# Binary cross-entropy on one core: other widths for the first and the last chunk, and another order of VectorE's work at the end

## The chip, the cores and the metric

The kernel runs on one core of one Trainium2 chip. The metric is the device time of one execution in microseconds. Its engines that matter here are VectorE (DVE), ScalarE (ACT), GpSimd (POOL) and SyncE (SP); TensorE has no work. Each engine takes its instructions in program order and waits where an operand isn't ready. Transfers between HBM (the large memory) and SBUF (the memory on the core: 128 partitions) are carried by 16 DMA engines; an engine's instruction issues a transfer, and here POOL issues nearly all of them.

## The reference

```python
def reference(pred, target):          # both 8192 x 8192, float32; target is 0 or 1
    eps = 1e-7
    pred = np.clip(pred, eps, 1 - eps)
    return -(target * np.log(pred) + (1 - target) * np.log(1 - pred))
```

268 MB are read for each of the two inputs, and 268 MB are written. As the target is 0 or 1, the result is -log(p) where it is 1 and -log(1 - p) where it is 0, that is -log(|p + t - 1|).

## The kernel before

The 8192 x 8192 elements are seen as one flat row, cut into 35 chunks. A chunk of width w takes 128 x w elements in a row: each of the 128 partitions holds w neighbouring ones. Chunks 1 to 33 have w = 15360 columns (`WIDE`), chunks 0 and 34 have 8704 (`SIDE`); per partition that makes 524288 columns.

Two buffers stand in SBUF. `ring_p` has three slots of 15360 float32 columns; chunk k lives in slot k mod 3, is loaded there, changed in place and stored from there. `ring_t` has one slot of 15360 columns of 8-bit integers for the target: the DMA reads float32 from HBM and writes 8-bit values, so a target load reads as many bytes as a pred load and writes a quarter.

Each chunk goes through these steps, in two halves (`PARTS`) of its columns:

- `load_p` (line 63) and `load_t` (line 67): loads of pred and target; all on POOL's queue but pred of chunk 0, which is on ACT's.
- `clip` (line 85): VectorE, a two-operation tensor_scalar, in place.
- `merge` (lines 89 to 95): VectorE computes (t - 1) + p (line 91); ScalarE takes the absolute value (line 94) and the logarithm (line 95), all in place.
- `negate` (line 99): VectorE multiplies by -1.
- `store` (line 70), and for the last chunk `store_last` (lines 72 to 81): all columns but the last 1024 in one transfer on POOL (line 74), the last 1024 in three transfers on SP, of 108, 12 and 8 rows (line 77).

The order is written out by hand (lines 101 to 128); a framework only adds the waits that the data needs, by the columns that two instructions share. For chunk k the program takes: merge of both halves; the target load of chunk k + 1, which waits until both merges have read `ring_t`; negate of both halves; clip of both halves of chunk k + 1; the store of chunk k; the pred load of chunk k + 2, which waits until the store of chunk k - 1 has emptied the slot. So POOL's queue is, from the start: t(0), p(1), t(1), store(0), p(2), t(2), store(1), p(3), and so on; an issue that waits holds up all that follow it. The DMA engines take POOL's transfers in the order of their issue.

At the end this changes. The store of chunk 32 isn't issued in its turn, but between the two halves of the target load of chunk 34 (lines 114 to 117): after t(33) and p(34), POOL has t(34, half 0), store(32), t(34, half 1), store(33), and the last store. VectorE takes for the last two chunks: merge(33) in both halves, negate(33) in both halves, clip(34), merge(34), negate(34).

Below p(k), t(k), store(k) are the transfers of chunk k, and merge(k, i), clip(k, i), negate(k, i) VectorE's work on half i.

Of the kernel before, what the change touches and what calls it, by code (L numbers as in the profile page):

```python
# [1 line left out]

# [4 lines left out]

EPS = 1e-7

WIDE = 15360  # L10
SIDE = 8704
SLOTS = 3
PARTS = 2
REST = 1024
ROWS = (108, 12, 8)


@with_exitstack
def kernel(
    ctx: ExitStack,  # L20
    tc: tile.TileContext,
    pred: bass.AP,
    target: bass.AP,
    out: bass.AP,
):
    nc = tc.nc
    fp32 = mybir.dt.float32
    uint8 = mybir.dt.uint8
    Alu = mybir.AluOpType
    Act = mybir.ActivationFunctionType  # L30
    P = nc.NUM_PARTITIONS

    R, C = pred.shape
    total = R * C // P
    n = (total - 2 * SIDE) // WIDE + 2
    widths = [SIDE] + [WIDE] * (n - 2) + [SIDE]
    assert sum(widths) == total
    last = n - 1

    pool = ctx.enter_context(tc.tile_pool(name="rings", bufs=1))  # L40
    ring_p = pool.tile([P, SLOTS * WIDE], fp32, name="ring_p", tag="ring_p")
    ring_t = pool.tile([P, WIDE], uint8, name="ring_t", tag="ring_t")
    warm = pool.tile([1, 8], fp32, name="warm", tag="warm")

    def chunk(ap, k):
        flat = ap.rearrange("r c -> (r c)")
        start = sum(widths[:k]) * P
        return flat[start : start + widths[k] * P].rearrange("(p w) -> p w", p=P)

    def p_of(k, a=0, b=None):  # L50
        c = k % SLOTS * WIDE
        return ring_p[:, c + a : c + (widths[k] if b is None else b)]

    def t_of(k, a=0, b=None):
        return ring_t[:, a : widths[k] if b is None else b]

    def part(k, i):
        w = widths[k]
        return i * w // PARTS, (i + 1) * w // PARTS

    def load_p(k):
        queue = nc.scalar if k == 0 else nc.gpsimd
        queue.dma_start(out=p_of(k), in_=chunk(pred, k))  # L63

    def load_t(k, *cols):
        cols = cols or (0, widths[k])
        nc.gpsimd.dma_start(out=t_of(k, *cols), in_=chunk(target, k)[:, cols[0] : cols[1]])  # L67

    def store(k):
        nc.gpsimd.dma_start(out=chunk(out, k), in_=p_of(k))  # L70

    def store_last():
        w = SIDE - REST
        nc.gpsimd.dma_start(out=chunk(out, last)[:, :w], in_=p_of(last, 0, w))  # L74
        r = 0
        for rows in ROWS:
            nc.sync.dma_start(
                out=chunk(out, last)[r : r + rows, w:], in_=p_of(last, w)[r : r + rows, :]
            )
            r += rows  # L80
        assert r == P

    def clip(k, i):
        p = p_of(k, *part(k, i))
        nc.vector.tensor_scalar(  # L85
            out=p, in0=p, scalar1=EPS, scalar2=1 - EPS, op0=Alu.max, op1=Alu.min
        )

    def merge(k, i):
        p, t = p_of(k, *part(k, i)), t_of(k, *part(k, i))  # L90
        nc.vector.scalar_tensor_tensor(  # L91
            out=p, in0=t, scalar=1.0, in1=p, op0=Alu.subtract, op1=Alu.add
        )
        nc.scalar.activation(out=p, in_=p, func=Act.Abs)  # L94
        nc.scalar.activation(out=p, in_=p, func=Act.Ln)  # L95

    def negate(k, i):
        p = p_of(k, *part(k, i))
        nc.vector.tensor_scalar(out=p, in0=p, scalar1=-1.0, scalar2=None, op0=Alu.mult)  # L99

    with tc.manual_schedule():
        load_p(0)
        load_t(0)
        load_p(1)
        nc.vector.memset(warm, 1.0)  # L105
        nc.scalar.activation(out=warm, in_=warm, func=Act.Ln)  # L106
        for i in range(PARTS):
            clip(0, i)
        for k in range(n):
            for i in range(PARTS):  # L110
                merge(k, i)
            if k < last - 1:
                load_t(k + 1)
            elif k == last - 1:
                load_t(last, 0, SIDE // PARTS)
                store(last - 2)
                load_t(last, SIDE // PARTS, SIDE)
            for i in range(PARTS):
                negate(k, i)
            if k < last:  # L120
                for i in range(PARTS):
                    clip(k + 1, i)
            if k < last - 2:
                store(k)
            if k < last - 1:
                load_p(k + 2)
        store(last - 1)
        store_last()


# [1 line left out]
_INS = ['pred', 'target']  # L132
_OUTS = [((8192, 8192), 'float32')]


# [23 lines left out]
```

## Time and profile before

| | us |
|---|---|
| median of 3 runs (1881.55 to 1883.01) | 1881.91 |
| the profiled execution, its own time | 1882.49 |
| its span, first to last instruction | 1880.5 |
| clip, L85, 7680 columns / 4352 columns, each | 4.16 / 2.42 |
| merge on VectorE, L91, 7680 / 4352, each | 8.15 / 4.68 |
| Abs, L94, and Ln, L95, 7680 / 4352, each | 6.60 / 3.82 |
| negation, L99, 7680 / 4352, each | 4.16 / 2.43 |
| POOL's issue of a target load, L67, mean of 36 | 0.53 |
| POOL's issue of a pred load, L63, mean of 34 | 3.88 |
| POOL's issue of a store, L70, mean of 34 | 3.74 |

The profile lists for each engine when it was busy, what ended its waits, and how busy the DMA engines were. A line of the timeline gives the start, the length, the engine, the line of the code, the operation, output and input by their names in the program, how many alike follow each other, and in brackets the idle time before it with what ended it. A line of the windows gives a stretch of time, its length, the busy time of VectorE, ScalarE and POOL in it (with the number of instructions), the clock, the mean busy share of the 16 DMA engines, and what they wrote in GB/s; a target load shows there with a quarter of the bytes that it reads.

### The profile page before, as it was taken

To read this page: it belongs to the slowest core of one execution; us is meant where nothing else is said; L and a number is where in the kernel's file an instruction comes from. 1 tells how busy PE (TensorE), PEld (TensorE's weight loads), DVE (VectorE), ACT (ScalarE), POOL (GpSimd) and SP (SyncE) were. 2 spreads that over 40 slices of the span, in tenths; PEclk is the share of its full clock that TensorE was granted. 3 is DMA by queue.
4 is the path that set the end of the run, shared out by engine and by line. 5 is a ranking of instruction groups with operands and counts; after the bars stand their busy time and mean duration, and the time that the engine had idled before them with its cause. 6 is when DMAs were issued, how large, how long until landed. Compare 5 with 4: busy or idle time off the path is not lost.

```text
span 1880.5 us, 651 instructions
## 1 busy us (share of the span) xinstructions
DVE 1116.4 (59%) x211; ACT 899.9 (48%) x142; POOL 278.6 (15%) x109
## 2 busy tenths in 40 slices
DVE  3666655655665566566655656665565566655654
ACT  3553335555443555544445554444555544445553
POOL 0111111101111110111111101111110111111000
DMA  9999999999999999999999999999999999999996
GB/s 301 304 357 295 312 306 303 328 360 359 308 311 311 306 312 356 360 337 303 307 312 312 334 358 354 311 305 306 312 319 359 358 323 311 306 306 312 349 293 268
DMA packets 15428, 604.02 MB, mean 321 GB/s; under 512 B 1728, under 2 KB 1728, under 8 KB 2112
## 3 DMA queue, kind: packets, MB, share of 16 engines
q0 software_dynamic: 15120, 599.01, 98.7%
q10 hardware_dynamic: 144, 4.46, 0.6%
q1 hardware_dynamic: 160, 0.52, 0.1%
q14 instruction: 4, 0.03, 0.0%
HBM read 536.87 MB, written 268.44 MB: 428 GB/s over the span
## 4 chain that ended last, share of the span: by engine, by line
DMA 65%; issue 30%; DVE 2%; ACT 1%; POOL 1%; POOLq 0%; DVEq 0%; PEldq 0%
DMA ring_t<-in_target_dram 65%; DVE ring_p L91 2%; ACT ring_p L95 1%; ACT ring_p L94 1%; POOL out_dram L70 0%; DVE ring_p L99 0%; POOL ring_p L63 0%; POOL ring_t L67 0%; POOLq L154 0%; POOLq L67 0%; POOLq L70 0%; DVEq L91 0%; PEldq L154 0%; POOLq L74 0%
## 5 line engine op out<-in xcount | busy, mean ns | idle before, releaser
L94 ACT ACTIVATE ring_p<-ring_p 128x7680 f32<-128x7680 f32 (+1 forms) x70 | 450.6, 6437 | 956.5 <-DVE ring_p L91 956.5
L91 DVE SCALAR_TENSOR_TENSOR ring_p<-ring_t,ring_p 128x7680 f32<-128x7680 uint8 (+1 forms) x70 | 554.0, 7956 | 239.1 <-DMA ring_t<-in_target_dram 239.1
L99 DVE TENSOR_SCALAR ring_p<-ring_p 128x7680 f32<-128x7680 f32 (+1 forms) x70 | 284.3, 4061 | 485.3 <-ACT ring_p L95 485.3
L95 ACT ACTIVATE ring_p<-ring_p 128x7680 f32<-128x7680 f32 (+1 forms) x70 | 451.1, 6444 | 2.2
L85 DVE TENSOR_SCALAR ring_p<-ring_p 128x7680 f32<-128x7680 f32 (+1 forms) x70 | 281.1, 4058 | 20.6 <-DMA ring_p<-in_pred_dram 20.6
L70 POOL DMA_DIRECT2D out_dram<-ring_p x34 | 127.2, 3742 | 716.5 <-DVE ring_p L99 716.5
L67 POOL DMA_DIRECT2D ring_t<-in_target_dram x36 | 19.1, 531 | 841.5 <-DVE ring_p L91 840.7
L63 POOL DMA_DIRECT2D ring_p<-in_pred_dram x34 | 131.8, 3877 | 1.3 <-DMA out_dram<-ring_p 1.3
L74 POOL DMA_DIRECT2D out_dram<-ring_p x1 | 0.5, 536 | 24.9 <-DVE ring_p L99 24.9
L106 ACT ACT_TABLE_LOAD x1 | 1.3, 1283 | 1.2 <-PEq L143 1.2
L105 DVE MEMSET warm<- 1x8 f32 x1 | 0.1, 65 | 0.8 <-PEq L143 0.8
L106 ACT ACTIVATE warm<-warm 1x8 f32<-1x8 f32 x1 | 0.2, 208 | 0.0
L143 POOL MEMSET const-float32-0.0<- 128x1 f32 x1 | 0.1, 98 | 0.2 <-issue 0.2
L143 POOL MEMSET const-bfloat16-1.0<- 128x1 bf16 x1 | 0.1, 102 | 0.0
L143 POOL MEMSET const-float32-1.0<- 128x1 f32 x1 | 0.1, 98 | 0.0
L143 POOL MEMSET const-uint8-127<- 128x1 uint8 x1 | 0.1, 98 | 0.0
## 6 DMA issues: line engine op xcount, KB each, us to landing
ring_p<-in_pred_dram POOLq DMA_DIRECT2D x33, 7680.0 KB, 47.6
out_dram<-ring_p POOLq DMA_DIRECT2D x33, 7680.0 KB, 33.4
ring_t<-in_target_dram POOLq DMA_DIRECT2D x33, 1920.0 KB, 37.7
ring_p<-in_pred_dram ACTq DMA_DIRECT2D x1, 4352.0 KB, 20.7
out_dram<-ring_p POOLq DMA_DIRECT2D x1, 4352.0 KB, 22.8
ring_p<-in_pred_dram POOLq DMA_DIRECT2D x1, 4352.0 KB, 46.2
out_dram<-ring_p POOLq DMA_DIRECT2D x1, 3840.0 KB, 12.9
ring_t<-in_target_dram POOLq DMA_DIRECT2D x1, 1088.0 KB, 22.8
```

The source lines that it names most:

```text
L63: queue.dma_start(out=p_of(k), in_=chunk(pred, k))
L67: nc.gpsimd.dma_start(out=t_of(k, *cols), in_=chunk(target, k)[:, cols[0] : cols[1]])
L70: nc.gpsimd.dma_start(out=chunk(out, k), in_=p_of(k))
L74: nc.gpsimd.dma_start(out=chunk(out, last)[:, :w], in_=p_of(last, 0, w))
L85: nc.vector.tensor_scalar(out=p, in0=p, scalar1=EPS, scalar2=1 - EPS, op0=Alu.max, op1=Alu.min)
L91: nc.vector.scalar_tensor_tensor(out=p, in0=t, scalar=1.0, in1=p, op0=Alu.subtract, op1=Alu.add)
L94: nc.scalar.activation(out=p, in_=p, func=Act.Abs)
L95: nc.scalar.activation(out=p, in_=p, func=Act.Ln)
L99: nc.vector.tensor_scalar(out=p, in0=p, scalar1=-1.0, scalar2=None, op0=Alu.mult)
L105: nc.vector.memset(warm, 1.0)
L106: nc.scalar.activation(out=warm, in_=warm, func=Act.Ln)
L143: nc = _bacc.Bacc("TRN2", target_bir_lowering=False, num_devices=1)
```

## The change

The number of chunks stays 35, and so does the width of the inner ones. The first chunk gets 4096 columns, the last 13312. The last store on POOL is cut in two: its first half of the columns (6656), and the rest up to the last 1024 (5632). The order of the work is the same up to chunk 32. For the last two chunks, POOL has both halves of the target load of chunk 34 ahead of store(32), and VectorE takes: merge(33, 0), merge(33, 1), clip(34, 0), clip(34, 1), negate(33, 0), merge(34, 0), negate(33, 1), merge(34, 1), negate(34, 0), negate(34, 1).

```diff
-SIDE = 8704
+FIRST = 4096
+FINAL = 13312
...
-    n = (total - 2 * SIDE) // WIDE + 2
-    widths = [SIDE] + [WIDE] * (n - 2) + [SIDE]
+    n = (total - FIRST - FINAL) // WIDE + 2
+    widths = [FIRST] + [WIDE] * (n - 2) + [FINAL]
...
     def store_last():
-        w = SIDE - REST
-        nc.gpsimd.dma_start(out=chunk(out, last)[:, :w], in_=p_of(last, 0, w))
+        half, w = FINAL // PARTS, FINAL - REST
+        for a, b in (0, half), (half, w):
+            nc.gpsimd.dma_start(out=chunk(out, last)[:, a:b], in_=p_of(last, a, b))
...
-        for k in range(n):
+        for k in range(last - 1):
             for i in range(PARTS):
                 merge(k, i)
-            if k < last - 1:
-                load_t(k + 1)
-            elif k == last - 1:
-                load_t(last, 0, SIDE // PARTS)
-                store(last - 2)
-                load_t(last, SIDE // PARTS, SIDE)
+            load_t(k + 1)
             for i in range(PARTS):
                 negate(k, i)
-            if k < last:
-                for i in range(PARTS):
-                    clip(k + 1, i)
+            for i in range(PARTS):
+                clip(k + 1, i)
             if k < last - 2:
                 store(k)
-            if k < last - 1:
-                load_p(k + 2)
+            load_p(k + 2)
+        for i in range(PARTS):
+            merge(last - 1, i)
+            load_t(last, *part(last, i))
+        store(last - 2)
+        for i in range(PARTS):
+            clip(last, i)
+        for i in range(PARTS):
+            negate(last - 1, i)
+            merge(last, i)
         store(last - 1)
+        for i in range(PARTS):
+            negate(last, i)
         store_last()
```

## The prediction

> **What bounds the kernel now.** I read the page first (busy time by engine, the DMA queues), then the DMA share by windows, then the timeline at both ends, and the groups kept apart by shape for durations.
>
> ```profile
> DVE 1116.4 (59%) x211; ACT 899.9 (48%) x142; POOL 278.6 (15%) x109
> q0 software_dynamic: 15120, 599.01, 98.7%
> ```
>
> No engine is near full; the transfers are. By windows (start:end, length, DVE, ACT, POOL busy, clock, DMA share, GB/s):
>
> ```profile
> 60.00:108.00 48.00, 32.48 (x6) 26.30 (x4) 8.17 (x3) 1.00 1.02 317
> 108.00:1800.00 1692.00, 1017.17 (x188) 815.37 (x124) 256.30 (x93) 1.00 1.00 326
> 1800.00:1810.00 10.00, 10.00 (x2) 5.39 (x1) 1.05 (x2) 1.00 0.72 165
> 1832.00:1840.00 8.00, 8.00 (x4) 0.00 (x0) 2.16 (x1) 1.00 0.85 182
> 1840.00:1852.00 12.00, 9.04 (x2) 7.49 (x2) 0.00 (x0) 1.00 1.14 492
> 1852.00:1866.00 14.00, 4.86 (x2) 7.72 (x3) 0.54 (x1) 1.00 0.38 147
> 1802.00:1804.00 2.00, 2.00 (x1) 0.00 (x0) 0.00 (x0) 1.00 0.45 192
> 1804.00:1806.00 2.00, 2.00 (x2) 1.39 (x1) 1.05 (x2) 1.00 0.08 35
> 1836.00:1838.00 2.00, 2.00 (x2) 0.00 (x0) 1.62 (x1) 1.00 0.14 13
> 1856.00:1863.00 7.00, 2.43 (x1) 3.75 (x1) 0.49 (x1) 1.00 0.00 0
> ```
>
> Up to 1800 us the share is 1.00 or more, so a busy engine there is covered. (Shares of short windows pass 1, as a packet counts where it starts; neighbours must be added.) All idle time is in the tail: 10 x 0.28 = 2.8 us around 1804, 8 x 0.15 = 1.2 us at 1837, and 14 x 0.62 - 12 x 0.14 = 7.0 us around 1860: together 11.0 us. The bytes don't change, so this is what can be won, and any new dry stretch is lost.
>
> The timeline says what runs dry, and gives the one delicate place at the head:
>
> ```profile
> 61.31 16.23 DVE L91 SCALAR_TENSOR_TENSOR ring_p<-ring_t,ring_p 128x7680 f32<-128x7680 uint8 x2 [4.54 <-DMA ring_t<-in_target_dram]
> 100.36 3.89 POOL L70 DMA_DIRECT2D out_dram<-ring_p  x1 [22.00 <-DVE ring_p L99]
> 1796.42 16.23 DVE L91 SCALAR_TENSOR_TENSOR ring_p<-ring_t,ring_p 128x7680 f32<-128x7680 uint8 x2 [7.48 <-DMA ring_t<-in_target_dram]
> 1804.87 0.53 POOL L67 DMA_DIRECT2D ring_t<-in_target_dram  x1 [43.97 <-DVE ring_p L91]
> 1835.46 2.16 POOL L70 DMA_DIRECT2D out_dram<-ring_p  x1 [21.99 <-DVE ring_p L99]
> 1859.78 2.43 DVE L99 TENSOR_SCALAR ring_p<-ring_p 128x4352 f32<-128x4352 f32 x1 [5.16 <-ACT ring_p L95]
> ```
>
> At 1804 the queue waits for merge(33,0) before target half 0 of chunk 34 may be loaded; at 1837 for POOL to issue store(33); at 1856 to 1863 nothing is left but the last store, which waits for the last merge, Abs, Ln and negation of chunk 34. POOL's issues take 0.53 us beside a merge, but 3.89 us when VectorE runs a clip (48.54 and 99.98 us, L85): there the issue ends with the clip.
>
> **The change, part by part.** *Rate.* From one target issue (1704.18) to the next (1758.57) a steady period is 54.4 us for three transfers of 15360 columns: 18.1 us each, so 4608 columns are 5.4 us of one transfer.
>
> *First chunk 4096.* p(0) and t(0) are 2 x 5.4 = 10.9 us shorter; this work is added again at the end, net nothing. The cost is store(0), also 5.4 us shorter. Before: t(1) landed by 61.3; behind it the queue held store(0) 10.3, p(2) 18.1 and t(2) 18.1 = 46.5 us, so it lasts until 107.8, less about 1 us between last byte and landing: 106.8. Store(1) can move from 100.36 + 3.89 + about 0.5 (after the issue that ended at 1837.62 the transfers start at about 1838.2) = 104.8. The margin is 2.0 us. After: the chain from t(1)'s landing to store(1) keeps its length (two merges, Abs and Ln twice, a negation, all of 7680 columns), the queue is 5.4 us shorter: 2.0 - 5.4 = a dry stretch of **3.4 us** at about 91 to 94 us. p(3) can't fill it, as it stands behind store(1) on POOL. Bounds: 0 if the issue took 0.53 (3.36 less, as beside merges), 5 if my two half-microsecond lags are off together. I take 3.4, by the row of this very issue. One period later store(1) is a full 18.1 instead of 4.8, so the margin is back at 7 to 10 us.
>
> The Trainium skill (SBUF — State Buffer, section "SBUF: two separate sides") says that VectorE in a two-port mode holds a port pair exclusively, and that GpSimd can't write descriptors meanwhile. The 3.89 against 0.53 us agree; by it the dry stretch is 3.4 us, without it 0.
>
> *Last chunk 13312 and the new order.* Durations for 6656 columns by the line through the two shapes of each row: clip or negation 3.6 (2427 ns at 4352, 4160 at 7680), merge 7.1 (4681, 8154), Abs or Ln 5.7 (3829, 6603). Everything up to t(33) is 10.9 + 5.4 us earlier and 3.4 later: t(33) lands at 1796.4 - 12.9 = 1783.5. p(34) follows with 15.7 us instead of 10.3, so the queue lasts to about 1796 (the first gap's mean, 1803.6, less 7.5). merge(33,0) ends at 1791.7: t(34,0), issued at 1792, is in time and the **2.8 us gap goes**. merge(33,1) ends at 1799.8; t(34,1) is issued then, on POOL ahead of store(32), and both now meet the clips of chunk 34 (1799.8 to 1807.0): 3.6 us each. t(34,0) takes 7.9 us, to 1804; t(34,1) can start at 1804.0. I price this at **0.3** (0 if p(34) lands a moment later and POOL is first, 0.9 for the engines that finish first); behind POOL waits store(32), ready at 1807.5 and needed at 1812.
>
> VectorE then: negate(33,0) to 1810.9, merge(34,0) to 1818.0, negate(33,1) to 1822.1 (its Ln ends at 1817.9), merge(34,1) to 1829.2. Store(33) is issued at 1822.5 beside a merge, while t(34,1) and store(32) occupy the queue to 1812 + 18.1 = 1830.2: the **1.2 us gap goes**, with 7 us to spare. negate(34,0) ends at 1833, negate(34,1) at 1845 (Abs and Ln of half 1 from 1829.5 to 1841); store(33) lasts to 1848.4, the first half of the last store 7.9 more: the **7.0 us gap goes**, with some 11 us to spare. The extra DMA and its issue (0.54, L74) lie beside these transfers; if that cover went they would cost 0.5.
>
> *What stays.* At the first gap the share fell over 4 us (0.45, then 0.08): the 16 engines end one transfer up to 3.5 us apart. Dry stretches let laggards catch up; with none, the lag stands at the end: **+1.5** (0 to 3; the split of the last 1024 columns is unchanged). And t(34,0) ran at 70 to 87 GB/s written (1806 to 1812) against 119 for a target load in the steady part, some 2 us; whether a load that isn't started from dry does so too the trace can't tell: **-1** (0 to -2).
>
> Sum: -11.0 + 3.4 + 0.3 + 1.5 - 1.0 = **-6.8 us**: the span 1880.5 becomes 1873.7; that profiled execution took 1882.49, 0.6 above the median of 1881.91, from which I subtract the same: **1875.1**. Bounds: -11 - 2 = -13 and -11 + 5 + 0.9 + 3 = -2.1.
>
> **Rivals.**
> 1. *No stall at the head* (the issue slips in before the clip): for it, 0.53 at 1804.87; against, 3.89 in exactly this place. -6.8 - 3.4 = -10.2: 1871.7. Chance 0.13.
> 2. *The gain is mostly given back* by a head stall of 5 and the full lag of 3 at the end: -6.8 + 1.6 + 1.5 = -3.7, 1878.2, within 0.2% (3.8 us, about what a measurement of this kernel can tell from no change). For it: laggards of 3.5 us; against: those are some engines of 16. Chance 0.11.
> 3. *Slower:* the stall at the head comes back each period, because a late store(k) delays p(k+2), a late p delays the clip, and this the merge that frees the target ring for the next load. Price 3.4 us a turn; from three more turns it is slower: -6.8 + 10.2 = +3.4, 1885.3. It decides where store(2) is ready later than t(3) ends. Against: clip(2) ends at 97, merge(2) starts there, store(2) is ready 43.5 later at 140.6, while store(1), p(3) and t(3) from 94 last to 148.4. For: that reserve is 8 us in a chain with six links. Chance 0.08.
> 4. *Each DMA has a fixed price.* If the start of every transfer cost the queue some 2 us, the extra one would: -4.8, 1877.1. Against: the share is 1.02 from 60 to 108, across four boundaries of transfers. Chance 0.04. The Trainium skill (DMA: Bandwidth & Descriptors, section "Anatomy of one DMA") fits about 2.0 us fixed per DMA; here queued transfers show none.
>
> That the order isn't the one said can't be: the program order is fixed by hand, and each engine takes it.
>
> **How the numbers follow.** Forecast 0.62, with the range 1873 to 1878 of its own; rivals 0.13, 0.11, 0.08, 0.04; what is left, 0.02, I halve between same and slower. Faster: 0.62 + 0.13 + 0.04 = 0.79; same 0.11 + 0.01 = 0.12; slower 0.08 + 0.01 = 0.09. The range leaves out the slow case and the far end of rival 1: 1870 to 1879.5.
>
> **What would show it.** DMA share: a dip of some 3 us between 88 and 96 us and none in the next period; no dip from 1790 to the end of the last transfers at about 1867; POOL's issue of store(1) near 89.5 us taking 3.9; t(34,1) issued beside a clip at about 3.6 instead of 0.53; the last negation (before: ended at 1862.2, 18 us ahead of the span's end) ending near 1845, some 29 us ahead of it. Wrong would be: more dips (rival 3), a last-store issue that finds the queue dry, or first transfers that take longer than 10 us for p(0) and t(0).

## The result and the profile after

Over 14 runs each, the changed kernel takes 1878.49 us in the median (1877.48 to 1879.8), the kernel before 1882.35 us (1881.49 to 1883.14): 3.9 us less, a ratio of 0.9980 with a 95% interval of 0.9972 to 0.9988. The profiled execution took 1878.88 us with a span of 1877.0 us, 3.5 us under the span before.

The windows of the changed kernel, with the columns as before (start:end, length, DVE, ACT and POOL busy, clock, DMA share, GB/s):

```profile
60.00:88.00 28.00, 13.80 (x3) 25.38 (x4) 0.53 (x1) 1.00 0.98 238
88.00:96.00 8.00, 8.00 (x3) 0.00 (x0) 6.07 (x2) 1.00 0.56 152
...
108.00:1790.00 1682.00, 1006.89 (x186) 813.24 (x124) 255.96 (x92) 1.00 1.00 325
...
1804.00:1808.00 4.00, 4.00 (x2) 4.00 (x2) 4.00 (x2) 1.00 0.86 78
1808.00:1850.00 42.00, 31.06 (x7) 35.57 (x6) 3.29 (x4) 1.00 1.01 368
1850.00:1862.00 12.00, 0.00 (x0) 0.00 (x0) 0.00 (x0) 1.00 0.95 410
1862.00:1867.00 5.00, 0.00 (x0) 0.00 (x0) 0.00 (x0) 1.00 1.02 439
1867.00:1872.00 5.00, 0.00 (x0) 0.00 (x0) 0.00 (x0) 1.00 0.35 149
```

The three dry stretches of the tail (11.0 us) are gone; a dip of 4 x 0.14 = 0.6 us is left at 1804 to 1808, and then the queue holds until the end. In their place stands a new one at the head: 8 x 0.44 = 3.5 us between 88 and 96 us. As a window counts a packet where it starts, the packets themselves give a better figure: a packet is one partition's part of a transfer, and each of the 16 engines ends its share of a transfer with a packet of 4 bytes. From the mean of these ends in t(2) to the mean start of store(1) it is 3.9 us.

The timeline of the same execution shows both:

```profile
50.89 16.23 DVE L93 SCALAR_TENSOR_TENSOR ring_p<-ring_t,ring_p 128x7680 f32<-128x7680 uint8 x2 [11.02 <-DMA ring_t<-in_target_dram]
...
89.93 3.89 POOL L71 DMA_DIRECT2D out_dram<-ring_p  x1 [21.99 <-DVE ring_p L101]
...
136.73 3.89 POOL L71 DMA_DIRECT2D out_dram<-ring_p  x1 [22.00 <-DVE ring_p L101]
...
1786.27 16.23 DVE L93 SCALAR_TENSOR_TENSOR ring_p<-ring_t,ring_p 128x7680 f32<-128x7680 uint8 x2 [7.47 <-DMA ring_t<-in_target_dram]
...
1794.72 0.53 POOL L68 DMA_DIRECT2D ring_t<-in_target_dram  x1 [43.97 <-DVE ring_p L93]
...
1802.79 3.36 POOL L68 DMA_DIRECT2D ring_t<-in_target_dram  x1 [7.54 <-DVE ring_p L93]
...
1825.31 0.54 POOL L71 DMA_DIRECT2D out_dram<-ring_p  x1 [15.62 <-DVE ring_p L101]
...
1843.70 3.63 DVE L101 TENSOR_SCALAR ring_p<-ring_p 128x6656 f32<-128x6656 f32 x1 [7.79 <-ACT ring_p L97]
```

The issue of store(1) meets the clip and takes 3.89 us; store(2) at 136.73 is in time again. At the end, t(34,1) meets a clip (3.36 us instead of 0.53), store(33) is issued beside a merge (0.54), and the last negation ends at 1847.3, 24 us before the last transfer.

What the forecast didn't have shows between the two ends. The target loads are issued at these times (start of POOL's issue, us):

| target load of chunk | 4 | 5 | 33 |
|---|---|---|---|
| before | 180.09 | 235.37 | 1758.57 |
| after | 168.04 | 223.04 | 1748.43 |
| earlier by | 12.0 | 12.3 | 10.1 |

The last column is from these lines, of before and then of after:

```profile
1758.57 0.53 POOL L67 DMA_DIRECT2D ring_t<-in_target_dram  x1 [23.90 <-DVE ring_p L91]
```

```profile
1748.43 0.53 POOL L68 DMA_DIRECT2D ring_t<-in_target_dram  x1 [23.90 <-DVE ring_p L93]
```

Three transfers that are 4608 columns shorter put everything behind them 3 x 5.4 = 16.3 us earlier. Of this 6.2 us are lost at t(33), where the idle time in the dip is 3.9 us.

### The profile page after: what moved, and what is told of

Its sections match the earlier page's. It is cut to its first block, busy times and chain, and to the rows that moved or that the text cites. A ratio compares the mean times of both kernels' runs of the same rounds, so it can differ in the third digit from the quotient of the medians.

```text
span 1877.0 us, 652 instructions
## 1 busy us (share of the span) xinstructions
DVE 1116.5 (59%) x211; ACT 899.8 (48%) x142; POOL 276.5 (15%) x110
## 4 chain that ended last, share of the span: by engine, by line
DMA 65%; issue 28%; ACT 3%; DVE 2%; POOL 0%; POOLq 0%; DVEq 0%; PEldq 0%
DMA ring_t<-in_target_dram 65%; DVE ring_p L93 2%; ACT ring_p L96 2%; ACT ring_p L97 1%; DVE ring_p L101 0%; POOL ring_p L64 0%; POOL out_dram L71 0%; POOLq L160 0%; POOL out_dram L76 0%; POOLq L68 0%; POOLq L71 0%; DVEq L93 0%; PEldq L160 0%
## 5 line engine op out<-in xcount | busy, mean ns | idle before, releaser
L96 ACT ACTIVATE ring_p<-ring_p 128x7680 f32<-128x7680 f32 (+2 forms) x70 | 450.5, 6436 | 940.5 <-DVE ring_p L93 940.5
L93 DVE SCALAR_TENSOR_TENSOR ring_p<-ring_t,ring_p 128x7680 f32<-128x7680 uint8 (+2 forms) x70 | 554.1, 7956 | 245.9 <-DMA ring_t<-in_target_dram 245.8
L101 DVE TENSOR_SCALAR ring_p<-ring_p 128x7680 f32<-128x7680 f32 (+2 forms) x70 | 284.3, 4061 | 467.0 <-ACT ring_p L97 467.0
L97 ACT ACTIVATE ring_p<-ring_p 128x7680 f32<-128x7680 f32 (+2 forms) x70 | 451.1, 6444 | 2.2
L87 DVE TENSOR_SCALAR ring_p<-ring_p 128x7680 f32<-128x7680 f32 (+2 forms) x70 | 281.1, 4058 | 17.1 <-DMA ring_p<-in_pred_dram 17.1
L71 POOL DMA_DIRECT2D out_dram<-ring_p x34 | 125.3, 3684 | 703.7 <-DVE ring_p L101 703.7
```

What stands on the lines that cost most here:

```text
L87: nc.vector.tensor_scalar(out=p, in0=p, scalar1=EPS, scalar2=1 - EPS, op0=Alu.max, op1=Alu.min)
L93: nc.vector.scalar_tensor_tensor(out=p, in0=t, scalar=1.0, in1=p, op0=Alu.subtract, op1=Alu.add)
```

## Experiments

Times are medians; "less" and "more" are against the kernel before on the same chip.

**The order alone and the widths alone.** First the new order, with the last store cut in two as in the change, and both outer chunks at 8704 columns:

```diff
-FIRST = 4096
-FINAL = 13312
+FIRST = 8704
+FINAL = 8704
```

> The new order of the last two chunks and the cut last store, with both outer chunks at the old 8704 columns. Theory A (the tail's dry stretches are what is won, and VectorE's order alone closes the long one): the gap at 1804 stays (2.6 us), t(34,1) is issued beside a clip and leaves a new gap of about 3.5 us at 1812 to 1816, the 7 us gap before the last store goes, nothing happens at the head: transfers end near 1869, span about 1875.5, 5.0 us less than before. Rival B (the wide last chunk is what covers the gaps, the order by itself is worth nothing): span 1880 to 1881.

And the kernel before with the new widths (the lines that use them follow suit):

```diff
-SIDE = 8704
+FIRST = 4096
+FINAL = 13312
...
```

> 4096 and 13312 columns, with the old order and the old single last store. Theory A: the stall at the head (3.8 us) is there, and at the end the last store waits until about 1866 for negate(34,1), while store(33) ends near 1852: a dry stretch of some 15 us; span about 1888, 7.5 us more than before. Rival B (the widths bring the gain): span 1877, 3.5 us less than before.

The order alone: 1878.0 us, 4.5 less (ratio 0.9976, 0.9966 to 0.9986), span 1876.3. The widths alone: 1890.66, 8.1 more (1.0044, 1.0032 to 1.0056), span 1888.7. Windows of the first, then of the second:

```profile
1804.00:1808.00 4.00, 4.00 (x2) 2.72 (x1) 0.53 (x1) 1.00 0.41 53
...
1812.00:1816.00 4.00, 4.00 (x3) 4.00 (x1) 2.39 (x2) 1.00 0.14 14
1816.00:1860.00 44.00, 24.29 (x7) 30.83 (x7) 3.72 (x4) 1.00 0.99 372
```

```profile
84.00:96.00 12.00, 10.77 (x3) 1.20 (x1) 6.32 (x2) 1.00 0.61 127
...
1848.00:1867.00 19.00, 7.25 (x2) 13.29 (x3) 0.54 (x1) 1.00 0.11 41
```

Theory A holds in both, gap by gap: the order takes away the long gap before the last store and brings one where t(34,1) waits for the clip; the wide last chunk without the order makes the last store wait 19 x 0.89 = 17 us by the window, 15.5 us by the packets. The whole change wins no more than the order alone (3.9 against 4.5 us, and the intervals overlap): the wide chunk closes the gaps that the order leaves, and the short first chunk gives as much back.

**Store(1) without the clip's delay, on SP.**

```diff
-        nc.gpsimd.dma_start(out=chunk(out, k), in_=p_of(k))
+        queue = nc.sync if k == 1 else nc.gpsimd
+        queue.dma_start(out=chunk(out, k), in_=p_of(k))
```

> The changed kernel with the store of chunk 1 alone issued from SP, whose issues no clip delays. Theory A (the dry stretch at 88 to 94 us costs its 3.8 us of idle time and some 2 us more, because all engines restart in step and cross the next ends of target loads together): no dip at 88 to 96 us, t(33) ends some 16 us earlier than before instead of 10.2, span about 1871.2, 5.8 us less than the changed kernel. Rival C (the 2 us lost after the stall come from the shifted rows in HBM, not from the restart): the idle time goes but t(33) ends only 14 us earlier, span about 1873.2. Rival D (a store on another queue than the loads is mixed with them and held up, so that the next load into its slot is late): span 1876 or more.

It settles nothing: 1879.69 us, with runs from 1871.8 to 1884.81, and the profiled one was among the long (span 1882.3). There the idle time at the head is gone, but p(3), no longer behind store(1) on POOL, is issued at 67.76 and the two queues are served in turn. By the packets of t(33), the 16 engines end it up to 9.7 us apart, against 4.1 us in the changed kernel, and the spread stays to the end, where it empties the queue:

```profile
84.00:108.00 24.00, 22.70 (x5) 3.57 (x2) 0.00 (x0) 1.00 0.96 344
...
1790.00:1800.00 10.00, 9.05 (x2) 0.86 (x1) 0.53 (x1) 1.00 0.74 319
1800.00:1816.00 16.00, 16.00 (x4) 15.97 (x3) 6.90 (x2) 1.00 0.86 102
```

The mixing that rival D named is there, and the time is on its side, but the late load that it named isn't: p(4) is issued at 140.44, right behind store(2), as in the changed kernel (140.62). What the shorter runs looked like wasn't profiled.

**Store(1) in halves, on POOL in its place.**

```diff
     def store(k):
-        nc.gpsimd.dma_start(out=chunk(out, k), in_=p_of(k))
+        for a, b in [part(k, i) for i in range(PARTS)] if k == 1 else [(0, widths[k])]:
+            nc.gpsimd.dma_start(out=chunk(out, k)[:, a:b], in_=p_of(k, a, b))
```

> The changed kernel with the store of chunk 1 in two halves, both on POOL in the same place: half 0 can be issued some 9 us before the end of t(2), half 1 follows. Theory A (the dry stretch at 91 to 94 us costs its 3.8 us and 2.3 us of restart): no dip at 88 to 96, t(33) ends about 16 us earlier than before instead of 10.2, span about 1871, 6 us less than the changed kernel, 10 less than before. Rival C (only the idle time is lost there, the rest comes from the rows' new places): span about 1873.2. Rival F (each transfer has a fixed price of 2 us, and there is one more): 2 us above either.

1872.09 us (1871.46 to 1873.65): 10.7 less than before (0.9944, 0.9931 to 0.9956), span 1870.0, the fastest kernel here. Timeline and windows:

```profile
76.38 0.54 POOL L72 DMA_DIRECT2D out_dram<-ring_p  x1 [8.87 <-DVE ring_p L102]
...
89.51 3.89 POOL L72 DMA_DIRECT2D out_dram<-ring_p  x1 [12.59 <-DVE ring_p L102]
```

```profile
88.00:96.00 8.00, 8.00 (x3) 0.00 (x0) 6.49 (x2) 1.00 0.98 336
96.00:108.00 12.00, 12.00 (x3) 2.55 (x1) 1.48 (x1) 1.00 1.03 443
```

```profile
1741.95 0.53 POOL L68 DMA_DIRECT2D ring_t<-in_target_dram  x1 [23.85 <-DVE ring_p L94]
```

Half 0 is issued at 76.38, and half 1, as slow as ever, lies beside its transfer. Theory A's number (1871) came out: t(33) is issued at 1741.95, 16.6 us before 1758.57 and 6.5 before the changed kernel, 2.6 more than the 3.9 us of idle time that went. The rows lie in HBM where they lie in the changed kernel, so rival C falls. One transfer more has no price that shows, so rival F falls too.

**The dip at the end.** In addition, the target load of chunk 34 is cut at column 7680:

```diff
-            load_t(last, *part(last, i))
+            load_t(last, *((0, WIDE // PARTS), (WIDE // PARTS, FINAL))[i])
```

> As store1_halves, and the target load of chunk 34 cut at column 7680 instead of 6656, so that its first part covers the wait of the second for the clip beside it. Theory A: the remaining dip at 1805 to 1807 (0.7 us) goes: span 0.7 less than store1_halves, about 1870.3. Rival: the slow packets at the end of these loads (1.8 us in sum) stay as they are and other engines' lag takes up the rest: no change.

1872.67 us (1871.74 to 1873.4), no different from 1872.09; 0.7 us could hardly show in runs up to 2.2 us apart. But in its trace the share between 1800 and 1804 us is 0.76, so the dip is still there, and theory A's way to close it failed. In this execution the engines end t(33) 5.9 us apart, against 4.0 with store(1) in halves alone, so the first of them run dry earlier; whether that is why, or the slow packets that the rival named, stays open.

**Other first chunks.**

```diff
-FIRST = 4096
-FINAL = 13312
+FIRST = 7424
+FINAL = 9984
```

> First chunk 7424, last 9984, new order. Theory A (the reserve of store(1) is worn out by 1.18 us for each 1000 columns less, and is nothing at about 7300): no dip at 88 to 96 us; at the end a gap of 1.4 us at 1800 and one of 3.3 us at 1810; span about 1874.4, 2.6 less than the changed kernel. Rival G (any shorter first chunk brings the restart loss): span 1876.5 or more.

And with 2048 and 15360:

> First chunk 2048, last 15360, new order. Theory A: a dry stretch of 3.8 + 2.4 = 6.2 us at about 86 to 93 us, the restart as in the changed kernel, nothing dry at the end: span about 1879, 2 us more than the changed kernel. Rival H (the restart loss grows with the length of the stretch, as 3.1 after 6.0 us against 2.3 after 3.8 us hints): span 1880. Rival I (the first loads of 8 KiB rows are slow): p(0) and t(0) take longer than 7 us together.

7424 takes 1879.36 us, 3.4 less than before, span 1877.4: rival G's side. Windows of it, then of 2048:

```profile
84.00:98.00 14.00, 5.03 (x2) 10.55 (x2) 0.00 (x0) 1.00 1.09 121
98.00:104.00 6.00, 6.00 (x3) 0.00 (x0) 4.93 (x2) 1.00 0.86 200
104.00:112.00 8.00, 8.00 (x2) 0.00 (x0) 3.04 (x1) 1.00 0.90 384
```

```profile
76.00:84.00 8.00, 3.30 (x1) 4.67 (x1) 0.00 (x0) 1.00 0.87 94
84.00:92.00 8.00, 8.00 (x3) 0.00 (x0) 6.84 (x2) 1.00 0.47 200
92.00:100.00 8.00, 8.00 (x2) 0.00 (x0) 1.13 (x1) 1.00 0.97 415
```

The reserve wasn't quite there: a dip remains at 98 to 112, 1.0 us by the packets. But t(33) is issued at 1757.92, where three transfers 1280 columns shorter (4.5 us) would put it at 1754.0: 3.9 us lost for 1 us of idle time. At the end it is dry for 4.8 us by the packets, about as expected (1.4 and 3.3). With 2048 the stretch is 5.6 us by the packets (expected 6.2). There t(33) is issued at 1744.63 instead of the 1735.0 that three transfers 6656 columns shorter would give: 9.6 us lost, 4.0 beyond the idle time. The time is 1878.92, 3.9 less than before and so no different from the changed kernel's, where theory A expected 2 us more. The dip at the tail (0.6 us) is gone; the rest of this difference isn't explained, and the profiled execution, with a span of 1878.5, was one of the longer ones. Its first loads are not slow: the packets of p(0) and t(0) lie between 1.8 and 7.7 us, 5.9 us where rival I named over 7. So the loss beyond the idle time is 2.9, 2.3 and 4.0 us behind stretches of 1.0, 3.9 and 5.6 us: it isn't in proportion to the stretch. That it doesn't come from the short chunk the next three test by themselves.

**One dry stretch in the middle of the kernel before,** by repeating the absolute value on chunk 16, which changes no value:

```diff
         nc.scalar.activation(out=p, in_=p, func=Act.Abs)
+        if k == 16:
+            nc.scalar.activation(out=p, in_=p, func=Act.Abs)
```

> The kernel before with one more Abs on each half of chunk 16 (it changes no value): store(16) comes 13.2 us later than in its neighbours, and as the reserve there is about 9.6 us, the DMA engines should run dry once for about 3.6 us near 930 us. Theory A: the loss is the idle time and about 2 us of restart in the next few periods: 5.5 us, span about 1886. Rival C: the idle time alone, 3.6 us, span about 1884. Rival E (engines that lag by up to 3.7 us catch up in the dry stretch): 2 us or less, span below 1882.5.

The same with a shorter and a longer delay (one repeat on half 0 and on 2560 columns of half 1; three repeats on half 0):

> The kernel before with one more Abs on half 0 of chunk 16 and on 2560 columns of half 1 (no value changes): store(16) 6.6 + 2.3 = 8.9 us late. In mid_dry 13.2 us made a stretch of about 6 us, so the reserve is about 7.2, and here the stretch should be some 1.7 us. Theory A' (a dry stretch costs its idle time and a fixed 2 to 3 us, since all engines start again in step, however short it was): span 4 to 5 us above before, 1884.5 to 1885.5. Rival H (the loss behind a stretch is in proportion to it, about half of it): 2.5 us, 1883. Rival E (lagging engines catch up): less than 1 us.

> The kernel before with three more Abs on half 0 of chunk 16 (no value changes): store(16) 19.8 us late, a dry stretch of about 12.6 us. Theory A': 12.6 + 3 = 15.6 us, span about 1896. Rival H (half as much again as the stretch): 19 us, span about 1899.5.

In the order short, middle, long they take 1887.62, 1892.19 and 1897.89 us: 5.8, 9.7 and 16.0 more. For the middle one 5.5 us were expected: its stretch came out at some 6 us instead of 3.6, as the reserve was smaller than reckoned. Windows of the short, the middle and the long one:

```profile
916.00:924.00 8.00, 7.64 (x2) 0.33 (x1) 3.19 (x1) 1.00 0.75 81
924.00:932.00 8.00, 8.00 (x3) 0.00 (x0) 4.78 (x2) 1.00 0.88 371
932.00:940.00 8.00, 8.00 (x2) 3.24 (x1) 0.00 (x0) 1.00 1.12 484
```

```profile
916.00:924.00 8.00, 2.98 (x1) 4.99 (x1) 0.00 (x0) 1.00 0.82 88
924.00:932.00 8.00, 8.00 (x3) 0.00 (x0) 6.53 (x2) 1.00 0.32 127
932.00:940.00 8.00, 8.00 (x2) 0.00 (x0) 1.44 (x1) 1.00 1.14 492
```

```profile
916.00:924.00 8.00, 1.98 (x1) 7.97 (x2) 0.00 (x0) 1.00 0.80 86
924.00:932.00 8.00, 5.05 (x2) 2.91 (x1) 0.60 (x1) 1.00 0.02 2
932.00:940.00 8.00, 8.00 (x3) 0.00 (x0) 7.37 (x2) 1.00 0.57 246
940.00:948.00 8.00, 8.00 (x2) 0.65 (x1) 0.00 (x0) 1.00 1.14 492
```

Idle time is 8 times the sum of what the shares lack of 1 (over 1 counts back); the loss is how much later the target load of chunk 32 is issued than in the kernel before (1704.18 there), less the offset that stood already at the issue of chunk 17's, ahead of the stretch (889.07 there). The issue for chunk 32, before and then in the short, the middle and the long one:

```profile
1704.18 0.53 POOL L67 DMA_DIRECT2D ring_t<-in_target_dram  x1 [23.85 <-DVE ring_p L91]
```

```profile
1709.60 0.53 POOL L67 DMA_DIRECT2D ring_t<-in_target_dram  x1 [23.85 <-DVE ring_p L91]
```

```profile
1713.82 0.53 POOL L67 DMA_DIRECT2D ring_t<-in_target_dram  x1 [23.80 <-DVE ring_p L91]
```

```profile
1719.98 0.53 POOL L67 DMA_DIRECT2D ring_t<-in_target_dram  x1 [23.85 <-DVE ring_p L91]
```

| | idle, us | loss at the issue, us | beyond the idle time, us |
|---|---|---|---|
| short | 2.0 | 1709.60 - 1704.18 - 0.22 = 5.2 | 3.2 |
| middle | 5.8 | 1713.82 - 1704.18 - 0.61 = 9.0 | 3.2 |
| long | 11.8 | 1719.98 - 1704.18 + 0.09 = 15.9 | 4.1 |

By the packets the idle time is 1.9, 6.1 and 12.3 us, and what is left 3.3, 2.9 and 3.6 us. A stretch six times as long costs about as much beyond its own length: 3 to 4 us. That is theory A', if a little more than the 2 to 3 us that it named; a loss in proportion (rival H) would be 1 and 6 us, and engines that catch up (rival E) would make it less than the idle time.

Where it is lost can be read in the packets. In the steady part a packet of an inner chunk takes 2.27 to 2.28 us. What the longer ones (over 2.29 us) take beyond that comes, from the end of t(17) to the end of t(31), to 0.1 us an engine in the kernel before, and to 3.1, 3.2 and 3.9 us in the short, the middle and the long one: with the idle time that is the whole loss, to 0.3 us. Up to 1740 us the same sum is 2.5 us in the kernel before, 4.6 in the changed kernel and 1.9 with store(1) in halves. So the kernel before pays this too, once: 2.3 of its 2.5 us lie in its first 600 us, in which its engines go from 0.8 to some 4 us apart.

It goes with how far apart the engines are. In the steady part they end a target load some 4 us apart (3.9 at the end of the kernel before, 4.0 to 4.4 ahead of the three stretches). Right behind a stretch all 16 start within 0.2 us of each other in the middle and the long one (in the short one, 14 of them), and end the next target load 0.8 and 0.7 us apart; the spread is back to about 3 us after some three periods in the short one, four in the middle one and eight in the long one. Some 2 us are lost in the period of the stretch itself, the rest in the next ones: by the engines' mean ends, the next four take 54.5 to 54.8 us each instead of 54.34.

The long packets lie where a store and a load meet. In the changed kernel, 16 packets each take up to 1.1 and 1.5 us longer at 108 to 112 us, just ahead of the end of store(1), behind which p(3) follows, and at 144 to 148 us, just ahead of the end of t(3), behind which store(2) follows. Between them, at 131 us, t(3) follows p(3), a load a load, and no packet is long. That it is the change in step which makes them slow is read from this; no experiment set the spread by itself.

## Why the prediction was right, and which terms were off

The forecast was 1875.1 us and faster; measured were 1878.49 us, faster by the path that was described. That is inside the range of 1870 to 1879.5 us, but half a microsecond above the 1873 to 1878 that the forecast gave for itself: it is the room left for the rivals that holds it, and the gain is little more than half of the one forecast. Term by term, in span: forecast -6.8, measured -3.5.

- *The tail's 11.0 us are won.* Right, and for the reasons given: t(34,0) was in time, store(33) was issued beside a merge at 1825.3, and the last negation ended long before it was needed.
- *A dry stretch of 3.4 us at 91 to 94 us.* Right in place, cause and length: 3.9 us by the packets (3.5 by the window), with L71's issue of 3.89 us beside the clip. That store(1) in two halves removes it shows the cause. The next period was in time, as worked out against rival 3.
- *What the stretch costs.* Here the sum was mis-sized: it priced a dry stretch at its idle time. The loss at t(33)'s issue is 6.2 us by shift and 6.5 by the experiment that removes it, 2.3 to 2.6 more than the idle time. The step said that dry stretches let laggards catch up, and they do: in the middle of the kernel the engines end 4.0 to 4.4 us apart ahead of a stretch and less than 1 us apart behind it. What it left out is that every such stretch costs some 3 us more behind it, until they are apart again.
- *+0.3 for t(34,1).* 0.6 by the window, the clip beside the issue as said.
- *+1.5 for the lag at the end.* By the packets the engines' mean end is 2.2 us ahead of the last one's, before 0.6: +1.6.
- *-1 for a target half that isn't started from dry.* Not there: by the packets the slow ones in these loads sum to 1.9 us an engine in both kernels. In the other transfers of the tail the kernel before has longer packets, 0.7 us an engine, and the changed kernel none.

With the measured terms: -11.0 + 3.9 + 2.3 + 0.6 + 1.6 - 0.7 = -3.3, against -3.5; the runs of the changed kernel lie within 1.3 us of their median. Rival 2 named nearly the measured time (1878.2), but by a stall of 5 and a lag of 3 us, which didn't occur. Rival 1 fell with the 3.89 us, rival 3 with the share of 1.00 from 108 us on, rival 4 with the faster kernel that has one transfer more. The Trainium skill's rule of the port that VectorE holds (SBUF — State Buffer, section "SBUF: two separate sides") agrees with each place here where a clip and an issue on POOL met: 3.89 and 3.36 us against 0.53.

## What to carry to other kernels

Where the transfers bound a kernel, add up the stretches in which the queue is dry, and price a new one at its length and, in this kernel, some 3 us more (2.3 to 4.0 us behind the six stretches of 1.0 to 12.3 us measured here). A shorter first chunk takes away cover one period later: compare the queue's content behind a load with the time until the next store can be issued. A store whose first half is ready early can be issued in halves; here that one line was worth more than the whole change.

## What was not expected of the hardware

The 16 DMA engines moved more when they were out of step: 54.34 us a period with ends some 4 us apart, 54.5 to 54.8 in the four periods after they were all started together. Out of step by more isn't better by itself: with ends 7 to 10 us apart, in the profiled run with store(1) on SP, the periods were 54.4 to 55.0 us throughout; with ends 5.9 us apart, in the run with the target load cut at column 7680, they were 54.34 again. Why the SP run stayed slower isn't shown.
